# A transformer block on one core: 96 instead of 80 tokens on gathered expert rows, and routing in two groups of four heads

## Chip, cores and metric

The kernel runs on one core of a Trainium2 chip. The metric is the device time of one execution in microseconds (us), as the median of three runs.

## What is computed

One block: two attention branches merged into `x`, then a product-key expert layer over 256 tokens of width 1024. The change touches only the expert layer:

```python
def peer_ffn(h, w_q, sub_k1, sub_k2, expert_u, expert_v):
    q = (ht @ w_q).reshape(T, PEER_HEADS, PEER_QDIM)
    s1 = jnp.einsum('thd,nd->thn', q[..., :PEER_HALF], sub_k1)
    s2 = jnp.einsum('thd,nd->thn', q[..., PEER_HALF:], sub_k2)
    v1, i1 = lax.top_k(s1, PEER_TOPK)
    v2, i2 = lax.top_k(s2, PEER_TOPK)
    cand = v1[..., :, None] + v2[..., None, :]
    vals, pos = lax.top_k(cand, PEER_TOPK)
    experts = jnp.take_along_axis(cand_idx, pos, axis=-1)
    gates = jax.nn.softmax(vals, axis=-1)
...
        u = expert_u[ec]
        a = jnp.einsum('cd,chkd->chk', xc, u)
        w = jax.nn.gelu(a) * gc
        return jnp.einsum('chk,chkd->cd', w, expert_v[ec])
```

There are 8 heads, 128 keys a side, 16 experts per head and token, and 16,384 experts with a row of 1024 float32 in `expert_u` and one in `expert_v`.

## The kernel before

The tokens are handled in two ways. For the last ND = 176 tokens every expert is computed: 128 tiles of U (128 experts by 1024, 512 KB) give `ps_u` (`u_tile`, L581), ScalarE applies gelu into `ga`, the gates multiply `ga`, and 128 tiles of V accumulate into `acc` (L833). Each U or V tile costs eight matmuls with 176 columns. For the first NG = 80 tokens only the chosen rows are fetched: an indirect DMA (`fetch`, L601) brings one row of `expert_u` to each of 128 partitions, VectorE forms the dot products (L617), and later the same with rows of `expert_v`, which it accumulates in `accG` (L627). SETS = (64, 16) says how the 80 tokens are laid on partitions: 64 tokens with two partitions each, 16 with eight. So 80 fetches of U rows and 80 of V rows are needed, 512 KB each.

The order of the work, all in `block_kernel`:

- Query: 16 tiles of `wq` give `qT` (L649 to L652). VectorE splits each weight tile into a high and a low part (L102), two to three tiles ahead.
- Routing: the generator `retrieval(h)` (L658) handles one half of 128 tokens and all eight heads: scores on TensorE (L667), a copy on ScalarE (L669), then on VectorE two rounds of top-16 and the one-hot sums that turn positions into expert numbers (`tri`); a softmax with an Exp on ScalarE (L728); for h = 0 small DMAs on SP's queue that lay indices and gates out for the gathers (`gidx`, `gwt`, L742); last, three transposes on TensorE (L746) and four copies.
- U, tiles 0 to 53 (`TOPK_TILES`): after each tile the loop L761 takes `TOPK_PER_TILE` = 1.4 units from the generator, whose `yield`s are the units' costs, and, once `gidx` is under way, `STEPS_U` = 0.85 steps of the generator `gathers` (L598). One step consumes one gathered row. The scheduler keeps each engine's queue in order, so what stands ahead in a queue holds what stands behind it.
- U, tiles 54 to 127: the same with `gate_group` (L780) for four tokens at a time: one-hot tiles, eight matmuls into `ps_g` (L797), and the product with `ga`.
- V, tiles 0 to 127: eight matmuls each, then `mark` (L835), a VectorE read of one column of the tile that keeps the gather steps behind it in VectorE's queue, then `STEPS_V` = 0.65 steps.

```python
        raw = wp.tile([P, DM], F32, name="uvraw", tag=("wraw", "whi", "wlo")[i % 3])
...
            if n % 2 == 1:
                for m in (n + 3, n + 4):
                    if m < 2 * NG:
                        fetch(m)
```

The first line gives weight tiles nine buffers, so SP loads up to nine ahead; a buffer is free again when TensorE and `mark` have read it. The others keep four gathered rows in flight or waiting, and two new ones are fetched when a pair is used up. SP issues the weight loads, POOL the indirect ones; both use the same 16 DMA engines.

Of the kernel before, what the change touches and what calls it, by code (L numbers as in the profile page):

```python
# [8 lines left out]
F32 = mybir.dt.float32  # L9
# [20 lines left out]
PH = 8  # L30
TOPK = 16
# [14 lines left out]
TOPK_PER_TILE = 1.4  # L46
# [20 lines left out]
def block_kernel(ctx: ExitStack, tc, x, g2, consts, small, wqkv, wkv5, wmg, w1kv, wup, wout, wq, uT, u, v, folds, out):  # L67
# [30 lines left out]
    state = {"tokens": 0, "tiles": 0}  # L98
# [482 lines left out]
    def u_tile(i, raw):  # L581
        ps = bank("ps_u", "u", 3)[:, :ND]
        for c in range(NC):
            nc.tensor.matmul(ps, raw[:, c * P:(c + 1) * P], h2f[:, c, NG:], start=c == 0, stop=c == NC - 1)  # L584
# [13 lines left out]
    def gathers():  # L598
        slots = []

        def fetch(n):  # L601
            src = u if n < NG else vrows
            if n % 2 == 0:
                slots.append(hpool.tile([P, 2, DM], F32, name="grow", tag="h2lo" if n // 2 % 2 else "h2hi"))
            dst = slots[n // 2][:, n % 2]
            j = n % NG
            nc.gpsimd.indirect_dma_start(out=dst, out_offset=None, in_=src,  # L607
                                         in_offset=bass.IndirectOffsetOnAxis(ap=gidx[:, j:j + 1], axis=0))

        for n in range(4):  # L610
            fetch(n)
        for n in range(2 * NG):
            g = slots[n // 2][:, n % 2]
            j = n % NG
            k = sum(j >= sum(SETS[:m]) for m in range(1, len(SETS)))
            if n < NG:
                nc.vector.tensor_tensor_reduce(out=g, in0=g, in1=h2d[k], scale=1.0, scalar=0.0, op0=ALU.mult,  # L617
                                               op1=ALU.add, accum_out=gdot[:, j:j + 1])
                if j % GCH == GCH - 1:
                    r = slice(j + 1 - GCH, j + 1)  # L620
                    nc.scalar.activation(gdot[:, r], gdot[:, r], AF.Gelu_apprx_tanh)
# [10 lines left out]
            yield  # L632
# [4 lines left out]
    def gather_steps(rate):  # L637
        gdebt[0] += rate
        while gdebt[0] >= 1:
            gdebt[0] -= 1  # L640
            with tc.issue_after(state["dve"].ins):
                next(gather, None)

    with ExitStack() as ts:
# [4 lines left out]
        for i in range(16):  # L649
            ps = bank("ps_q", "u", 3)[:, :S]  # L650
            cols_proj(wq[i], ps, lambda c: (h2hi[:, c, :], h2lo[:, c, :]), lo_last=i == 0)
            nc.scalar.copy(qT[:, i, :], ps)  # L652

# [4 lines left out]
        def retrieval(h):  # L658
            sp = tk
            vals = sp.tile([P, 2, PH, TOPK], F32, name="tv")  # L660
            idx = sp.tile([P, 2, PH, TOPK], U32, name="ti")
            for w in range(2):
                sc = sp.tile([P, PH, P], F32, name="sc12")
                for q in range(2):
                    ps = pst.tile([P, 512], F32, name="ps_s12", tag="t", bufs=3).rearrange("p (h n) -> p h n", n=P)
                    for k in range(4):
                        nc.tensor.matmul(ps[:, k, :], qT[:, 2 * (4 * q + k) + w, h * P:(h + 1) * P],  # L667
                                         SM("k2T" if w else "k1T"), start=True, stop=True, skip_group_check=True)
                    nc.scalar.copy(sc[:, 4 * q:4 * q + 4], ps)  # L669
                yield 0.0  # L670
                for hh in range(PH):
                    state["dve"] = topk(nc, sp, vals[:, w, hh, :], idx[:, w, hh, :], sc[:, hh, :], P)
                    yield 1.0
            idf = sp.tile([P, 2, PH, TOPK], F32, name="idf")
            nc.vector.tensor_copy(idf, idx)
            cand = sp.tile([P, PH, NCAND], F32, name="cand")
            o = a = 0
            while a < TOPK:
# [15 lines left out]
            off = sp.tile([P, P], F32, name="off")
            inc = sp.tile([P, P], F32, name="inc")
# [7 lines left out]
            pb = sp.tile([P, P], F32, name="pb")  # L703
            nc.vector.tensor_sub(pb, pa, off)
            nc.vector.scalar_tensor_tensor(pb, pa, float(o + CAND_N[TOPK // 2 - 1]), pb, op0=ALU.is_lt, op1=ALU.mult)
            yield 2.6
            diff = sp.tile([P, PH, TOPK], F32, name="diff")
            nc.vector.tensor_copy(diff[:, :, 0:1], idf[:, 0, :, 0:1])
            nc.vector.tensor_sub(diff[:, :, 1:], idf[:, 0, :, 1:], idf[:, 0, :, :TOPK - 1])
            for w, (pos, op, table) in enumerate(((pa, ALU.is_ge, diff), (pb, ALU.is_equal, idf[:, 1]))):  # L710
                posb = sp.tile([P, PH, TOPK], BF16, name="posb")
                nc.vector.tensor_copy(posb.rearrange("p h j -> p (h j)"), pos)
                for q in range(2):
                    hs = slice(4 * q, 4 * q + 4)
                    oh = sp.tile([P, 4, TOPK, TOPK], BF16, name="oh", tag="oh")
                    nc.vector.tensor_tensor(oh, posb[:, hs].unsqueeze(2).to_broadcast([P, 4, TOPK, TOPK]),
                                            steps16[:, w].unsqueeze(1).to_broadcast([P, 4, TOPK, TOPK]), op=op)
                    nc.vector.tensor_mul(oh, oh, table[:, hs].unsqueeze(3).to_broadcast([P, 4, TOPK, TOPK]))
                    o2 = sp.tile([P, 4, TOPK // 2, TOPK], BF16, name="oh2", tag="oh2")
                    nc.vector.tensor_add(o2, oh[:, :, 0::2], oh[:, :, 1::2])  # L720
                    nc.vector.tensor_add(oh[:, :, 0:4], o2[:, :, 0::2], o2[:, :, 1::2])
                    nc.vector.tensor_add(o2[:, :, 0:2], oh[:, :, 0:4:2], oh[:, :, 1:4:2])
                    state["dve"] = nc.vector.tensor_add(tri[:, w, hs], o2[:, :, 0], o2[:, :, 1])
                    yield 2.6
            ex = sp.tile([P, PH, TOPK], F32, name="ex")
            nc.vector.tensor_sub(ex, tv, tv[:, :, 0:1].to_broadcast([P, PH, TOPK]))
            with tc.issue_after(state["act"].ins):
                nc.scalar.activation(ex, ex, AF.Exp)  # L728
            se = sp.tile([P, PH], F32, name="se")
            nc.vector.tensor_reduce(se, ex, axis=AX.X, op=ALU.add)  # L730
            nc.vector.reciprocal(se, se)
            nc.vector.scalar_tensor_tensor(tri[:, 2], ex, GSCALE, se.unsqueeze(2).to_broadcast([P, PH, TOPK]),
                                           op0=ALU.mult, op1=ALU.mult)
            if h == 0:
                tf = tri.rearrange("p i h j -> p i (h j)")
                ei = sp.tile([P, P], U32, name="ei")
                nc.vector.scalar_tensor_tensor(ei, tf[:, 0], float(NKEY), tf[:, 1], op0=ALU.mult, op1=ALU.add)
                for dst, src in ((gidx, ei), (gwt, tf[:, 2])):
                    for k, n in enumerate(SETS):
                        o = sum(SETS[:k])  # L740
                        for i in range(P // n):
                            nc.sync.dma_start(dst[i * n:(i + 1) * n, o:o + n], src[o:o + n, i * n:(i + 1) * n])  # L742
                state["rows"] = True
            pt = bank("ps_tri", "g")[:, :3 * P].rearrange("p (i t) -> p i t", t=P)
            for i in range(3):
                nc.tensor.transpose(pt[:, i, :], tri[:, i].rearrange("p h j -> p (h j)"), C("ident"))  # L746
# [221 lines left out]
```

## Time and profile before

| | us |
|---|---|
| median of 3 runs (lowest, highest) | 980.64 (980.05, 981.41) |
| profiled execution | 977.79 |
| its span, first to last instruction | 975.9 |
| TensorE busy in the span | 950.0 |
| VectorE busy | 577.1 |

The mean granted clock of TensorE is 0.993 of full speed. Over the span DMA moved 265 MB, 272 GB/s. Busy shares are means over stages that differ, so the stretches are read one by one. In the rows below PE is TensorE, PEld its weight loads, DVE VectorE, ACT ScalarE, POOL GpSimd, and SP the engine that issues the weight loads.

### The profile page before, as it was taken

The numbers are of one execution on the slowest core, as the hardware profiler recorded it, in microseconds if no ns is written. First come the engines' busy times: TensorE is split into PE (matmuls) and PEld (weight loads), VectorE is DVE, ScalarE is ACT, GpSimd is POOL, SyncE is SP. The second block draws the span as 40 slices with busy tenths as digits, with TensorE's granted clock in tenths as the row PEclk, the third lists the DMA queues.
The fourth block names the chain that finished last, engine by engine and source line by source line (L and its number), as shares of the span: only waits on it lengthen the run. The fifth ranks groups of instructions, "written<-read, shape, count | busy, mean of one in ns | idle before, by whom it ended". The sixth has DMA issues, their size and how long they took to land.

```text
span 975.9 us, 16945 instructions
## 1 busy us (share of the span) xinstructions
PE 950.0 (97%) x6465; PEld 903.5 (93%) x6465; DVE 577.1 (59%) x1575; ACT 313.6 (32%) x787; POOL 179.8 (18%) x185
## 2 busy tenths in 40 slices
PE   8999999999999999869999999999999999999998
PEld 6778758997999999869999999999999999999997
DVE  5887775586428849976777777764444344343201
ACT  6777776546431121025444544420000000000000
POOL 2000000002000023332232333224332323232000
PEclk9999999999999999989999999999999999999999
DMA  7665302567576589987999999999999999999751
GB/s 240 191 220 188 117 1 96 186 198 195 161 248 200 172 308 401 356 283 273 332 322 338 323 323 328 343 324 389 399 387 381 358 376 346 370 365 378 233 177 44
DMA packets 74448, 265.15 MB, mean 272 GB/s; under 512 B 9152, under 2 KB 9408, under 8 KB 74368
## 3 DMA queue, kind: packets, MB, share of 16 engines
q1 hardware_dynamic: 50512, 177.61, 51.4%
q0 software_dynamic: 23856, 86.47, 25.1%
q8 instruction: 51, 0.84, 0.3%
q14 instruction: 29, 0.24, 0.1%
HBM read 261.86 MB, written 1.05 MB: 269 GB/s over the span
## 4 chain that ended last, share of the span: by engine, by line
PE 86%; DVE 5%; DMA 5%; ACT 2%; issue 1%; POOL 0%; SPq 0%; ACTq 0%
PE acc L833 31%; PE ps_u L584 26%; PE ps_g L797 4%; DMA grow<-in_u_dram,gidx 2%; PE ps_q L117 2%; PE ps_mg L120 2%; PE ps_mg L117 2%; PE ps_q L118 2%; PE ps_mg L118 2%; PE ps_s L406 2%; PE ps_q L120 1%; DMA wraw<-in_wqkv_dram 1%; DVE grow L617 1%; PE ps_proj L167 1%; PE ps_pt L423 1%; PE ps_proj L165 1%
## 5 line engine op out<-in xcount | busy, mean ns | idle before, releaser
L584 PE MATMUL ps_u<-h2f,uvraw 128*128 128x176 f32 x2048 | 319.4, 316 | 2.6 <-ACT ga L588 2.6
L584 PEld LDWEIGHTS ps_u<-h2f,uvraw 128*128 128x128 f32 x2048 | 311.1, 193 | 2.9 <-ACT ga L588 2.8
L833 PE MATMUL acc<-ga,uvraw 128*128 128x176 f32 x2048 | 305.7, 313 | 0.0
L833 PEld LDWEIGHTS acc<-ga,uvraw 128*128 128x128 f32 x2048 | 305.5, 190 | 0.0
L607 POOL DMA_INDIRECT grow<-in_u_dram,gidx x80 | 85.8, 1073 | 296.8 <-DVE gdot L617 150.9
L102 DVE TENSOR_TENSOR wlo<-wraw,whi 128x1024 fp32r<-128x1024 f32 (+1 forms) x80 | 95.6, 1197 | 42.5 <-ACT whi L101 42.1
L627 DVE SCALAR_TENSOR_TENSOR accG<-grow,gwt,accG 128x1024 f32<-128x1024 f32 x78 | 99.9, 1281 | 35.0 <-DMA grow<-in_v_dram,gidx 34.6
L607 POOL DMA_INDIRECT grow<-in_v_dram,gidx x80 | 81.9, 1024 | 188.9 <-DVE accG L627 113.6
L835 DVE COPY mark<-uvraw 128x1 f32<-128x1 f32 x128 | 19.5, 152 | 150.2 <-DMA uvraw<-in_v_dram 147.2
L617 DVE CUSTOM_DVE_ANT_0 grow<-grow,h2d 128x1024 f32<-128x1024 f32 x80 | 97.4, 1218 | 12.5 <-DMA grow<-in_u_dram,gidx 12.2
L101 ACT CAST whi<-wraw 128x1024 fp32r<-128x1024 f32 (+1 forms) x80 | 82.0, 1029 | 67.8 <-PE ps_q L118 18.4
L846 ACT COPY accT<-acc 128x352 f32<-128x352 f32 x2 | 0.9, 452 | 304.7 <-PE acc L833 304.7
L588 ACT ACTIVATE ga<-ps_u 128x176 f32<-128x176 f32 (+35 forms) x124 | 33.9, 275 | 181.9 <-PE ps_u L584 170.2
L792 ACT ACTIVATE og<-o,gT 128x128 f16<-128x128 f16 x176 | 67.3, 566 | 17.4 <-PE ps_g L797 14.2
L797 PE MATMUL ps_g<-og,o 128*128 128x128 f16 x352 | 48.5, 295 | 0.0
L592 DVE TENSOR_TENSOR ga<-ga,au 128x176 f32<-128x176 f32 (+35 forms) x74 | 18.8, 255 | 41.2 <-ACT au L591 36.4
L797 PEld LDWEIGHTS <-o 128*128 128x128 f16 x352 | 40.0, 116 | 2.0
L164 PE MATMUL ps_proj<-whi,hhi 128*128 128x512 f32 (+1 forms) x96 | 36.4, 382 | 2.3 <-ACT whi L101 1.5
L165 PE MATMUL ps_proj<-whi,hlo 128*128 128x512 f32 (+1 forms) x96 | 35.7, 377 | 0.0
L117 PE MATMUL ps_mg<-hhi,whi 128*128 128x256 f32 x128 | 32.3, 288 | 0.0
L117 PE MATMUL ps_q<-h2hi,whi 128*128 128x256 f32 x128 | 31.6, 284 | 0.7 <-ACT qTp L652 0.5
L118 PE MATMUL ps_mg<-hlo,whi 128*128 128x256 f32 x128 | 31.9, 285 | 0.0
(256 smaller groups left out, 1103.6 us busy)
## 6 DMA issues: line engine op xcount, KB each, us to landing
uvraw<-in_uT_dram SPq DMA_DIRECT2D x128, 512.0 KB
uvraw<-in_v_dram SPq DMA_DIRECT2D x128, 512.0 KB
wraw<-in_wqkv_dram SPq DMA_DIRECT2D x20, 512.0 KB
wraw<-in_wmg_dram SPq DMA_DIRECT2D x16, 512.0 KB
wraw<-in_wq_dram SPq DMA_DIRECT2D x16, 512.0 KB
wraw<-in_w1kv_dram SPq DMA_DIRECT2D x8, 512.0 KB
wraw<-in_wup_dram SPq DMA_DIRECT2D x8, 512.0 KB
wraw<-in_wout_dram SPq DMA_DIRECT2D x8, 512.0 KB
```

The source lines that it names most:

```text
L101: nc.scalar.copy(hi, src)
L102: state["dve"] = nc.vector.tensor_sub(lo, src, hi)
L117: nc.tensor.matmul(ps, lh, rh, start=i == 0, stop=False)
L118: nc.tensor.matmul(ps, ll if lo_last else lh, rh if lo_last else rl, start=False, stop=False)
L165: nc.tensor.matmul(ps(h), ll, hi[:, r], start=False, stop=False)
L584: nc.tensor.matmul(ps, raw[:, c * P:(c + 1) * P], h2f[:, c, NG:], start=c == 0, stop=c == NC - 1)
L607: nc.gpsimd.indirect_dma_start(out=dst, out_offset=None, in_=src, in_offset=bass.IndirectOffsetOnAxis(ap=gidx[:, j:j + 1], axis=0))
L617: nc.vector.tensor_tensor_reduce(out=g, in0=g, in1=h2d[k], scale=1.0, scalar=0.0, op0=ALU.mult, op1=ALU.add, accum_out=gdot[:, j:j + 1])
L627: nc.vector.scalar_tensor_tensor(accG[:, k], g, gwt[:, j:j + 1], accG[:, k], op0=ALU.mult, op1=ALU.add)
L792: nc.scalar.activation(og[0][:, :, k], o1[:, :, k], AF.Copy, scale=gT[:, t0 + k:t0 + k + 1])
L797: nc.tensor.matmul(ps[:, k, :], o2[:, :, k], og[i][:, :, k], start=i == 0, stop=i == 1, skip_group_check=True)
L833: nc.tensor.matmul(acc[c // 2][:, c % 2, 0:ND], raw[:, c * P:(c + 1) * P], ga_at(i), start=i == 0 and c % 2 == 0, stop=i == NKEY - 1, skip ...
```

## The change

- NG becomes 96 (SETS = (64, 32)), so ND becomes 160 and each fetch count 96. Matmuls on `u` and `acc` have 160 columns, there are 40 gate groups instead of 44.
- `retrieval(h, hg, tri)` handles four heads (QH = 4) and runs four times. The first two groups belong to h = 0, and each lays out its own half of `gidx` and `gwt`; `state["rows"]` says how many fetches are covered, and `gather_steps` stays six behind it until all are.
- The generator starts beside query tile 8 (`TOPK_PER_Q` = 1.0 a tile), then takes 1.1 units per U tile, over 60 tiles instead of 54. Gather steps: 0.55 a tile in these, 0.8 in the other U tiles, 0.9 in V.
- The transposes and copies become `route(h, tri)`. That of h = 0 is emitted after the third group, that of h = 1 two units after the fourth, each behind the latest U matmul.

```diff
-TOPK_TILES = 54
-SETS = (64, 16)
+TOPK_TILES = 60
+SETS = (64, 32)
...
-STEPS_U = 0.85
-STEPS_V = 0.65
+STEPS_R = 0.55
+STEPS_U = 0.8
+STEPS_V = 0.9
...
-TOPK_PER_TILE = 1.4
+TOPK_PER_TILE = 1.1
+TOPK_PER_Q = 1.0
...
     def gather_steps(rate):
-        gdebt[0] += rate
-        while gdebt[0] >= 1:
+        gdebt[0] += rate if "rows" in state else 0.0
+        while gdebt[0] >= 1 and (state["rows"] == NG or state["steps"] + 6 <= state["rows"]):
             gdebt[0] -= 1
+            state["steps"] += 1
...
+        def route(h, tri):
+            with tc.issue_after(state["pe"].ins):
+                pt = bank("ps_tri", "g")[:, :3 * P].rearrange("p (i t) -> p i t", t=P)
+                for i in range(3):
+                    nc.tensor.transpose(pt[:, i, :], tri[:, i].rearrange("p h j -> p (h j)"), C("ident"))
...
         def both():
+            tris = [tk.tile([P, 3, PH, TOPK], F32, name="tri") for _ in range(NH)]
             for h in range(NH):
-                yield from retrieval(h)
+                for hg in range(HG):
+                    yield from retrieval(h, hg, tris[h])
+                    if h == 1 and hg == 0:
+                        route(0, tris[0])
+                        yield 0.8
+            yield 2.0
+            route(1, tris[1])
+            yield 0.8
...
+        for i in range(16):
+            ps = bank("ps_q", "u", 3)[:, :S]
+            cols_proj(wq[i], ps, lambda c: (h2hi[:, c, :], h2lo[:, c, :]), lo_last=i == 0)
+            state["act"] = nc.scalar.copy(qT[:, i, :], ps)
+            if i >= PH:
+                topk_steps(TOPK_PER_Q)
...
             u_tile(i, ahead.pop(0))
-            debt -= TOPK_PER_TILE
...
-            if "rows" in state:
-                gather_steps(STEPS_U)
+            topk_steps(TOPK_PER_TILE)
+            gather_steps(STEPS_R)
```

TensorE's queue at the end of the routing, before. `ps_s` are scores, `ps_u` U tiles (eight rows each), `ps_tri` the transposes, `o_...` the first weights of a gate group:

```order
L667 MATMUL ps_s_4043<-sml,qTp 128x128 x4
L667 MATMUL ps_s_4049<-sml,qTp 128x128 x4
L584 MATMUL ps_u<-h2f,uvraw 128x176 x152
L746 MATMUL ps_tri<-cst,tri 128x128 x2
L584 MATMUL ps_u<-h2f,uvraw 128x176 x12
L746 MATMUL ps_tri<-cst,tri 128x128
L584 MATMUL ps_u<-h2f,uvraw 128x176 x12
L797 LDWEIGHTS o_4562
```

And with the change:

```order
L588 MATMUL ps_u<-h2f,uvraw 128x160 x96
L751 MATMUL ps_tri<-cst,tri 128x128 x3
L588 MATMUL ps_u<-h2f,uvraw 128x160 x8
L668 MATMUL ps_s_4341<-sml,qTp 128x128 x4
L588 MATMUL ps_u<-h2f,uvraw 128x160 x24
L668 MATMUL ps_s_4409<-sml,qTp 128x128 x4
L588 MATMUL ps_u<-h2f,uvraw 128x160 x112
L751 MATMUL ps_tri<-cst,tri 128x128 x3
L588 MATMUL ps_u<-h2f,uvraw 128x160 x8
L819 LDWEIGHTS o_4745
```

The transposes of h = 0 now stand far behind their group's scores, with the third group's U tiles between; those of h = 1 stand together, one U tile ahead of the first gate group.

SP's queue from the first U loads to the first V load, before (`gidx` and `gwt` are the small transfers that lay indices and gates out):

```order
L578 DMA uvraw<-in_uT_dram 128x1024 x26
L742 DMA gidx<-ei 64x64 x2
L742 DMA gidx<-ei 16x16 x8
L578 DMA uvraw<-in_uT_dram 128x1024 x9
L742 DMA gwt<-tri 64x64 x2
L742 DMA gwt<-tri 16x16 x8
L578 DMA uvraw<-in_uT_dram 128x1024 x93
```

And with the change:

```order
L582 DMA uvraw<-in_uT_dram 128x1024 x12
L743 DMA gidx<-ei 64x32 x2
L743 DMA gidx<-ei 32x16 x4
L582 DMA uvraw<-in_uT_dram 128x1024 x6
L743 DMA gwt<-tri 64x32 x2
L743 DMA gwt<-tri 32x16 x4
L582 DMA uvraw<-in_uT_dram 128x1024 x14
...
L582 DMA uvraw<-in_uT_dram 128x1024 x2
...
L582 DMA uvraw<-in_uT_dram 128x1024 x94
```

The first `gidx` stands behind 12 loads instead of 26, and a second set of small transfers (left out) follows behind 32 and 34 loads.

## Rows read from the trace of the kernel before

**Rows 1.** The page: busy time per engine (share) xinstructions; the chain's shares by line.

```profile
PE 950.0 (97%) x6465; PEld 903.5 (93%) x6465; DVE 577.1 (59%) x1575; ACT 313.6 (32%) x787; POOL 179.8 (18%) x185
...
PE acc L833 31%; PE ps_u L584 26%; PE ps_g L797 4%; DMA grow<-in_u_dram,gidx 2%; PE ps_q L117 2%; PE ps_mg L120 2%; PE ps_mg L117 2%; PE ps_q L118 2%; PE ps_mg L118 2%; PE ps_s L406 2%; PE ps_q L120 1%; DMA wraw<-in_wqkv_dram 1%; DVE grow L617 1%; PE ps_proj L167 1%; PE ps_pt L423 1%; PE ps_proj L165 1%
```

**Rows 2.** Windows: stretch, length, busy time per engine (instructions), clock, DMA share, GB/s.

```profile
370.00:395.00 25.00, 25.00 (x173) 25.00 (x173) 23.56 (x130) 4.34 (x12) 6.70 (x7) 1.00 1.02 400
657.00:697.00 40.00, 40.00 (x270) 40.00 (x270) 19.66 (x30) 0.63 (x2) 16.43 (x16) 1.00 1.01 387
700.00:740.00 40.00, 40.00 (x270) 40.00 (x269) 17.64 (x32) 0.00 (x0) 12.95 (x12) 1.00 1.01 390
...
288.06:435.00 146.94, 135.60 (x910) 134.59 (x910) 112.36 (x551) 28.25 (x69) 30.84 (x27) 0.97 0.82 293
...
659.50:965.00 305.50, 305.50 (x2050) 305.50 (x2049) 107.47 (x198) 0.77 (x2) 72.65 (x72) 1.00 0.89 331
```

**Rows 3.** TensorE's groups and the waits at the end of the routing.

```profile
L746 PE MATMUL ps_tri<-cst,tri 128*128 128x128 f32 x6 | 1.8, 325 | 8.8 <-DVE tri L732 7.5 <-DVE tri L723 1.2
...
PE ps_u L584 <- ACT ga L588: 2.6, 1, 2.6
```

**Rows 4.** The chain in order of time (start, us, what) at 424 us.

```profile
424.68 8.36 DMA grow<-in_u_dram,gidx
...
434.44 0.30 DVE tri L732
...
434.79 0.47 PE ps_tri L746
```

**Rows 5.** Waits from 659.5 to 965 us (total, times, longest).

```profile
DVE mark L835 <- DMA uvraw<-in_v_dram: 143.8, 84, 4.6
...
DVE accG L627 <- DMA grow<-in_v_dram,gidx: 34.6, 22, 4.9
```

**Rows 6.** VectorE's timeline: the first mark of V.

```profile
645.76 0.15 DVE L835 COPY mark<-uvraw 128x1 f32<-128x1 f32 x1 [2.50 <-DMA uvraw<-in_v_dram]
```

**Rows 7.** The chain in order of time: query, U, scores, gates, V, the end.

```profile
287.10 0.96 PE ps_q L120 x8
288.06 2.39 PE ps_u L584 x16
290.45 1.78 PE ps_s L667 x16
...
444.78 0.94 PE ps_g L797 x8
...
659.52 305.49 PE acc L833 x2048
965.01 3.43 PE fin L843 x8
968.44 3.59 PE fin L850 x32
```

**Rows 8.** VectorE's windows beside the query tiles and in L617 alone; two of its groups.

```profile
260.00:288.06 28.06, 9.21 (x8) 1.00 0.63 202
...
357.80:435.00 77.20, 29.63 (x49) 0.95 0.91 339
...
L702 DVE TENSOR_TENSOR off<-off,inc 128x128 f32<-128x128 f32 x12 | 3.4, 284 | 0.0
...
L723 DVE TENSOR_TENSOR tri<-oh 128x64 f32<-128x64 bf16 x8 | 1.7, 218 | 0.0
```

**Rows 9.** The DMA view from 700 to 860 us.

```profile
DMA packets 16184, 59.06 MB, mean 369 GB/s; under 512 B 1795, under 2 KB 1795, under 8 KB 16172
```

**Rows 10.** Windows of 1 us, TensorE alone: around two waits; busy time, clock, DMA share, GB/s.

```profile
238.00:239.00 1.00, 0.00 (x0) 1.00 0.92 206
...
240.00:241.00 1.00, 0.76 (x8) 1.00 0.98 127
...
408.00:409.00 1.00, 1.00 (x5) 0.50 1.00 397
```

More of the change, by code (lines that the diff above doesn't have):

```diff
@@ L30 @@
 PH = 8
+HG = 2
+QH = PH // HG
 TOPK = 16
@@ L96, in block_kernel @@
     x1 = hpool.tile([P, NH, DM], F32, name="x1")
-    state = {"tokens": 0, "tiles": 0}
+    state = {"tokens": 0, "tiles": 0, "steps": 0}
     def split(hi, lo, src):
@@ L583, in u_tile @@
         for c in range(NC):
-            nc.tensor.matmul(ps, raw[:, c * P:(c + 1) * P], h2f[:, c, NG:], start=c == 0, stop=c == NC - 1)
+            state["pe"] = nc.tensor.matmul(ps, raw[:, c * P:(c + 1) * P], h2f[:, c, NG:], start=c == 0, stop=c == NC - 1)
         dst = ga_at(i)
@@ L614, in gathers @@
             j = n % NG
-            k = sum(j >= sum(SETS[:m]) for m in range(1, len(SETS)))
+            k = sum(j % (NG // HG) >= sum(SETS[:m]) // HG for m in range(1, len(SETS)))
             if n < NG:
@@ L623, in gathers @@
                                                    op0=ALU.mult, op1=ALU.mult)
-            elif j == sum(SETS[:k]):
+            elif k not in begun:
+                begun.add(k)
                 nc.vector.tensor_scalar(accG[:, k], g, gwt[:, j:j + 1], None, op0=ALU.mult)
@@ L648, in block_kernel @@
         qT = tk.tile([P, 16, S], F32, name="qTp", bufs=1)
[L649 to L652, printed above, removed]
         steps16 = tk.tile([P, 2, TOPK, TOPK], BF16, name="steps16", bufs=1)
@@ L709, in retrieval @@
             nc.vector.tensor_sub(diff[:, :, 1:], idf[:, 0, :, 1:], idf[:, 0, :, :TOPK - 1])
+            hs = slice(QH * hg, QH * hg + QH)
             for w, (pos, op, table) in enumerate(((pa, ALU.is_ge, diff), (pb, ALU.is_equal, idf[:, 1]))):
-                posb = sp.tile([P, PH, TOPK], BF16, name="posb")
+                posb = sp.tile([P, QH, TOPK], BF16, name="posb")
                 nc.vector.tensor_copy(posb.rearrange("p h j -> p (h j)"), pos)
[L713 to L724, printed above, removed]
@@ new lines, in retrieval @@
+                o2 = sp.tile([P, QH, TOPK // 2, TOPK], BF16, name="oh2", tag="oh2")
+                nc.vector.tensor_add(o2, oh[:, :, 0::2], oh[:, :, 1::2])
+                nc.vector.tensor_add(oh[:, :, 0:4], o2[:, :, 0::2], o2[:, :, 1::2])
+                nc.vector.tensor_add(o2[:, :, 0:2], oh[:, :, 0:4:2], oh[:, :, 1:4:2])
+                state["dve"] = nc.vector.tensor_add(tri[:, w, hs], o2[:, :, 0], o2[:, :, 1])
+                yield 2.2
+            ex = sp.tile([P, QH, TOPK], F32, name="ex")
@@ L733, in retrieval @@
                                            op0=ALU.mult, op1=ALU.mult)
             if h == 0:
[L735 to L738, printed above, removed]
+                ei = sp.tile([P, QH, TOPK], U32, name="ei")
+                state["dve"] = nc.vector.scalar_tensor_tensor(ei, tri[:, 0, hs], float(NKEY), tri[:, 1, hs],
+                                                              op0=ALU.mult, op1=ALU.add)
@@ L739, in retrieval @@
+                for dst, src in ((gidx, ei), (gwt, tri[:, 2, hs])):
+                    src = src.rearrange("p h j -> p (h j)")
                     for k, n in enumerate(SETS):
-                        o = sum(SETS[:k])
+                        o, m = sum(SETS[:k]), n // HG
+                        c = hg * (NG // HG) + o // HG
                         for i in range(P // n):
-                            nc.sync.dma_start(dst[i * n:(i + 1) * n, o:o + n], src[o:o + n, i * n:(i + 1) * n])
-                state["rows"] = True
@@ L744, in retrieval @@
-            pt = bank("ps_tri", "g")[:, :3 * P].rearrange("p (i t) -> p i t", t=P)
-            for i in range(3):
-                nc.tensor.transpose(pt[:, i, :], tri[:, i].rearrange("p h j -> p (h j)"), C("ident"))
+                            nc.sync.dma_start(dst[i * n:(i + 1) * n, c:c + m], src[o:o + n, i * m:(i + 1) * m])
+                state["rows"] = (hg + 1) * NG // HG
+            yield 0.4
+        def route(h, tri):
[3 more added lines that the diff above has]
+                    nc.tensor.transpose(pt[:, i, :], tri[:, i].rearrange("p h j -> p (h j)"), C("ident"))
```

77 lines of the change are left out of this document (40 added, 37 removed).

## The prediction

> **What bounds the kernel now.** I read the page first, then the windows by stage, then the chain, then the waits and the DMA views.
>
> TensorE is busy for 97% of the span, and two lines carry over half of the chain that ended last [rows 1]: `acc` L833 with 31% and `ps_u` L584 with 26%. The reader is to see there that only shorter TensorE work, or fewer stalls of it, can shorten this kernel. Both multiply weight tiles by 176 columns of tokens. The trace has 2,048 passes for a stage of 128 tiles [rows 7], sixteen a tile, so one matmul of the code is two passes.
>
> The windows by stage [rows 2] show two kinds of stretch. From 659.5 to 965.0 us (the V stage: `acc`) TensorE is never idle. In the stretch that holds the routing, from 288.06 to 435 us, it is busy for 135.6 of 146.9 us, and its mean clock is 0.97. What ended those idle times is in the waits [rows 3]: the routing transposes L746 waited 7.5 and 1.2 us for VectorE's `tri`, and `ps_u` waited 2.6 us for ScalarE, in whose queue a step waits for VectorE's dot products. The chain at 424 us [rows 4] says why VectorE was late: it waited 8.4 us for a gathered row that stands in its queue ahead of the last softmax step. So the first U tiles are bound by VectorE and its gathers, the rest by TensorE's columns.
>
> What nearly binds as well is DMA. In V it moves 331 GB/s over the whole stage, and in its filled stretches 387 and 390 GB/s at a share of 1.01 [rows 2]. VectorE's waits in V are for transfers [rows 5]: `mark` waits 143.8 us for weight tiles, which is harmless because they land ahead of their use. The first mark stands at 645.76 us [rows 6], V's first matmul at 659.52 [rows 7]: 13.8 us, some six tiles ahead.
>
> **The change, part by part.**
>
> *Columns.* ND falls from 176 to 160. A pass takes 305.49 us / 2048 = 149.2 ns at 176 columns; the same float32 passes take 3.43 / 8 = 429 ns at 512 columns and 3.59 / 32 = 112 ns at 128 [rows 7]. On the line from 176 to 512 sixteen columns are worth 13.3 ns, on the line from 128 to 176 12.3. I take the first, since it is nearer to what a clean stream pays: 135.9 ns, a tile of 2.174 us where it was 2.387. That is 27.3 us less in U (25.2 by the other line) and, if TensorE stays the bound, 27.3 us less in V.
>
> *Gate groups.* 40 groups of four tokens instead of 44, at 0.94 us of TensorE each [rows 7]: 3.8 us less. Scores and transposes keep their number.
>
> *The routing stall.* U runs from 288.06 to 659.52 us [rows 7], 371.5 us. In it lie 2048 x 149.2 ns = 305.5, 44 x 0.94 = 41.4, 64 score passes at 1.78 / 16 = 7.1, and six transposes at 0.3 = 1.8 [rows 3, 7]. What is left, 16 us, is stalls and the slow clock behind them. The change starts VectorE's routing beside the query tiles, where VectorE is now busy for 9.2 of 28.1 us [rows 8], and queues each half's transposes later. VectorE's work before the last transposes: 112.4 us busy in that stretch less 29.6 us of gathers [rows 2, 8] = 83 us of routing, plus some 4 us (an estimate: 33 small steps a group, issued four times rather than twice, at about 60 ns of fixed cost, from 284 ns at 128 elements and 218 at 64 [rows 8]), plus 28 gathers at 1.2 us and eight splits at 1.2 us [rows 8]: 130 us. The time for it, from query tile 8 to the transposes behind U tile 58, is 8 x 2.88 us (24 passes at 0.96 / 8 [rows 7]) + 59 x 2.174 + 8 for scores = 159 us. So it fits, with less room near the end, where five reductions stand ahead of the last softmax step, each behind a gather. I leave 5 us of the 16; bounds 0 and 16. Saved: 11 us. The cover here is that room; if gathers take it, the last transposes are late again.
>
> *Queues.* SP now issues the first index transfers after 12 U loads and not 26, and sits behind `ei` with the 13th load. `ei` of the first group is due near U tile 5 and tile 12 is used 26 us after U's start, so I cost it at nothing. POOL meets `accT`'s memset after 86 gathers rather than 90; the 87th row is wanted at the tenth mark of V, so this waits for nothing new. Four Exp table changes instead of two are ScalarE's, busy for 28 of 147 us there [rows 2].
>
> *More gathers.* Each of 192 rows (before 160) is 0.524 MB like a weight tile. By the rates in the code 28 are used in the first 60 U tiles and 55 in the other 68, so 83 by the end of U (before 88 of 160), and 109 are left for V at 0.9 a tile, the last at V tile 121. In U this needs at most 1.55 x 0.524 MB / 2.174 us = 374 GB/s: it just fits. In V it needs 1.9 x 0.524 / 2.174 = 458 GB/s, and that does not fit: the highest rate that these stretches hold is 400, for 25 us [rows 2]. So V, today bound by TensorE, becomes bound by DMA.
>
> Its length: at V's start some six tiles have landed and 87 rows are fetched. To V tile 121 that leaves 116 tiles and 105 rows, 221 x 0.5243 = 115.9 MB. At 393 GB/s, between the filled 40 us stretches (387, 390) and the 25 us one (400), it is 295 us; then come the landing and six to seven tiles at 2.174, 15 us: 310 us. Bounds: 305 at 400 GB/s, 314.5 at 387. Against 305.5 now, V gets 4.5 us *longer* though its matmuls are 27.3 us shorter. VectorE, busy for 107 of 305.5 us there now [rows 2], has room for half as many steps again.
>
> Here a rule speaks against the change. The Trainium skill (DMA: Bandwidth & Descriptors, Specifications) gives about 358 GB/s as one core's share of HBM; by that the 115.9 MB take 324 us, V 339 and the run 972 us. The trace differs from it, with 387 to 400 GB/s held, so it has no part in my sum.
>
> *Sum.* 975.9 (span) - 27.3 - 3.8 - 11 + 4.5 = 938.3 us of span. The profiled execution took 977.8 us, 1.9 more than its span, so 940.2; the median of the runs shown, 980.64, is 2.85 above it, so **943 us** in the runs.
>
> **Rivals.**
>
> *TensorE stays the bound in V.* V takes 128 x 2.174 = 278 us, 32 less: 911 us. For it: weights are now ready six tiles ahead. Against: it needs 458 GB/s for 265 us, and no stretch holds that.
>
> *DMA in V holds only its mean.* From 700 to 860 us it moved 369 GB/s at shares near full [rows 9]. At that 115.9 MB take 314 us, V 329: 962 us. For it: random rows and weight tiles mix as they do there. Against: there the gathers were paced by VectorE's marks, so the engines were not always asked.
>
> *Routing late again.* The last transposes wait as now, for gathers ahead of the softmax step: 16 us of stall instead of 5, 954 us. For it: the 8.4 us gather of [rows 4], in a stage that will ask for 374 GB/s. Against: the room of 29 us worked out above.
>
> *Slower: the clock falls in V.* TensorE will wait for weights in V for the first time. After its wait of 2.6 us near 404 us [rows 3] the granted clock was 0.50 (1.2 GHz) in the window at 408 us [rows 10]. At 1.2 GHz a tile takes 4.35 us, longer than the 2.5 us between transfers, so TensorE would bind and lose time. With V at 349 us the gain is used up: that is when 26% of its tiles run at the low level; at 35%, V takes 376 us and the run 1009. Against: the waits come to 32 us over 128 tiles, mostly 0.4 us a tile, and after a wait of about 2 us near 238.5 us the clock stayed at 1.00 [rows 10]. The Trainium skill (TensorE: Matmul & The Clock Gate, HAM oscillation) describes this failure for loops that wait on DMA at every step; the two rows show one wait with it and one without.
>
> **Chances.** My forecast, V bound by DMA near 393 GB/s and a small stall: 0.62 (933 to 959 us by its bounds). TensorE-bound V 0.08; DMA at its mean 0.12; late routing 0.14; clock 0.04. The range reaches from 920 to 962: it holds the forecast, late routing and most of the case at 369 GB/s, and leaves out TensorE-bound V and the clock. A measurement of this kernel can tell about 0.2% from no change, 2 us. Faster by more than that are all cases but the last: 0.94; a mild form of the clock case lands within 0.2%: 0.02; slower 0.04.
>
> **What would show it.** In the changed profile: about 136 ns per pass where nothing waits; V between 305 and 315 us, with TensorE idle in it by some 30 us put down to `uvraw` from the V table; DMA near 390 GB/s from V's start to its last gather, and VectorE's `mark` waiting far less than 143.8 us, its accumulations far more than 34.6 [rows 5]. U should be near 329 us, and the transposes should wait for `tri` by under 5 us. I am wrong about DMA if V takes 280 us or 330, about the clock if the granted clock in V is below 0.95, and about routing if the transposes wait over 10 us.

## The result, and the profile after

| | before | after |
|---|---|---|
| median of the runs made side by side (lowest, highest) | 980.35 (978.66, 981.41) | 941.18 (938.46, 945.49) |
| profiled execution | 977.79 | 938.46 |
| its span | 975.9 | 936.7 |

The ratio is 0.9606, with a 95% interval of 0.9567 to 0.9645. The forecast was 943 us with a range of 920 to 962. Where the time went is a sum of four stretches, each from the first matmul of one stage to that of the next. After the change they are read here, in the view of single lines (durations min/median/max in ns, first and last start in us):

```profile
L588 PE MATMUL ps_u<-h2f,uvraw x2048: 297/299/317, 289.2 to 611.1; 128*128 128x160 f32 x187
...
L855 PE MATMUL acc<-ga,uvraw x2048: 299/299/403, 611.2 to 925.2; 128*128 128x160 f32 x187
```

| stretch | before [rows 7] | after | difference |
|---|---|---|---|
| up to U | 288.06 | 289.2 | +1.1 |
| U | 371.5 | 322.0 | -49.5 |
| V | 305.5 | 314.2 | +8.7 |
| end of V to end of span | 10.9 | 11.3 | +0.4 |

So U gave 49 us, V gave 9 us back. The page of the changed kernel (busy time per engine, then the chain that ended last, by engine and by line) answers to [rows 1]:

```profile
PE 900.6 (96%) x6433; PEld 842.9 (90%) x6433; DVE 614.3 (66%) x1663; ACT 309.6 (33%) x768; POOL 218.4 (23%) x213
...
PE 56%; DMA 28%; issue 7%; POOL 3%; DVE 3%; ACT 2%; DVEq 0%; POOLq 0%; ACTq 0%; SPq 0%
PE ps_u L588 28%; DMA grow<-in_v_dram,gidx 21%; PE ps_g L819 4%; POOL grow L611 3%; DMA grow<-in_u_dram,gidx 3%; PE ps_q L121 2%; PE ps_mg L124 2%; PE ps_mg L121 2%; PE ps_q L124 2%; PE ps_q L122 2%; PE ps_mg L122 2%; PE ps_s L410 2%; PE ps_proj L171 1%; PE ps_pt L427 1%; DVE wlo L106 1%
```

Before, `acc` alone carried 31% of the chain. Now the chain of V runs over DMA: `grow` from the V table carries 21% of the span, and `acc` is no longer among the leading lines. The groups (busy us, mean ns of one, idle time before them and its releaser) say the same from TensorE's side:

```profile
L855 PE MATMUL acc<-ga,uvraw 128*128 128x160 f32 x2048 | 292.9, 302 | 21.3 <-DMA uvraw<-in_v_dram 19.5
L855 PEld LDWEIGHTS acc<-ga,uvraw 128*128 128x128 f32 x2048 | 279.9, 190 | 34.2 <-DMA uvraw<-in_v_dram 32.3
L588 PE MATMUL ps_u<-h2f,uvraw 128*128 128x160 f32 x2048 | 287.3, 299 | 0.0
...
L751 PE MATMUL ps_tri<-cst,tri 128*128 128x128 f32 x6 | 1.0, 273 | 0.0
```

The last two rows have no idle time at all: the transposes, which waited 8.8 us [rows 3], wait for nothing, and neither does `ps_u`. By stage (length, busy time per engine, clock, DMA share, GB/s), beside [rows 2]:

```profile
289.00:430.00 141.00, 141.00 (x1051) 140.68 (x1050) 118.55 (x546) 39.02 (x97) 34.33 (x32) 1.00 0.92 349
430.00:611.00 181.00, 181.00 (x1376) 179.72 (x1375) 137.38 (x370) 89.33 (x321) 54.67 (x52) 1.00 0.95 345
...
660.00:700.00 40.00, 37.15 (x262) 35.46 (x261) 19.12 (x29) 0.00 (x0) 15.55 (x14) 1.00 0.95 362
700.00:900.00 200.00, 183.82 (x1271) 173.61 (x1269) 96.48 (x151) 0.00 (x0) 80.14 (x72) 1.00 1.01 394
...
611.00:926.00 315.00, 293.67 (x2053) 280.45 (x2052) 151.63 (x254) 1.37 (x4) 119.80 (x109) 1.00 0.99 385
```

TensorE is never idle in U, and the clock is 1.00 in all these stretches, V's idle times included. Over 200 us of V, DMA moves 394 GB/s, over all of V 385. The waits (total, times, longest):

```profile
DVE accG L633 <- DMA grow<-in_v_dram,gidx: 136.9, 93, 3.7
...
PEld acc L855 <- DMA uvraw<-in_v_dram: 32.3, 51, 2.2
```

VectorE's accumulations wait 136.9 us where they waited 34.6, and `mark`, which waited 143.8 [rows 5], no longer stands among the long waits (3.4 us in all). What paces V now is in the chain in order of time, from 718 to 740 us:

```profile
717.99 8.72 DMA grow<-in_v_dram,gidx
...
726.81 0.06 DVE accG L633
726.87 1.14 issue
728.01 0.16 DVE mark L857
...
728.36 0.94 POOL grow L611
729.30 0.30 issue
729.60 7.41 DMA grow<-in_v_dram,gidx
...
739.90 7.44 DMA grow<-in_v_dram,gidx
```

This is a closed loop: rows land, VectorE adds them, POOL fetches the next pair into the buffers, they land. One turn takes 11.6 and 10.3 us. Two pairs turn at once, so four rows per turn, 2.6 to 2.9 us a row. The rows by VectorE's lines (first and last start at the end; L631 takes the first row of each of the two sets):

```profile
L633 DVE SCALAR_TENSOR_TENSOR accG<-grow,gwt,accG x94: 1283/1285/1346, 657.7 to 922.6; 128x1024 f32<-128x1024 f32 x94
L631 DVE TENSOR_SCALAR accG<-grow,gwt x2: 752/752/753, 655.7 to 745.3; 128x1024 f32<-128x1024 f32 x2
```

One of the two rows of L631 lies between the first and the last of L633, so 264.9 us hold 94 rows: 2.82 us a row. It is counted so in every run below.

### The profile page after: what moved, and what is told of

The parts are those of the page before. It is cut to its first block, busy times and chain, and to the rows that moved or that the text cites. A ratio compares the mean times of both kernels' runs of the same rounds, so it can differ in the third digit from the quotient of the medians.

```text
span 936.7 us, 17034 instructions
## 1 busy us (share of the span) xinstructions
PE 900.6 (96%) x6433; PEld 842.9 (90%) x6433; DVE 614.3 (66%) x1663; ACT 309.6 (33%) x768; POOL 218.4 (23%) x213
## 4 chain that ended last, share of the span: by engine, by line
PE 56%; DMA 28%; issue 7%; POOL 3%; DVE 3%; ACT 2%; DVEq 0%; POOLq 0%; ACTq 0%; SPq 0%
PE ps_u L588 28%; DMA grow<-in_v_dram,gidx 21%; PE ps_g L819 4%; POOL grow L611 3%; DMA grow<-in_u_dram,gidx 3%; PE ps_q L121 2%; PE ps_mg L124 2%; PE ps_mg L121 2%; PE ps_q L124 2%; PE ps_q L122 2%; PE ps_mg L122 2%; PE ps_s L410 2%; PE ps_proj L171 1%; PE ps_pt L427 1%; DVE wlo L106 1%
## 5 line engine op out<-in xcount | busy, mean ns | idle before, releaser
L855 PE MATMUL acc<-ga,uvraw 128*128 128x160 f32 x2048 | 292.9, 302 | 21.3 <-DMA uvraw<-in_v_dram 19.5
L855 PEld LDWEIGHTS acc<-ga,uvraw 128*128 128x128 f32 x2048 | 279.9, 190 | 34.2 <-DMA uvraw<-in_v_dram 32.3
L588 PE MATMUL ps_u<-h2f,uvraw 128*128 128x160 f32 x2048 | 287.3, 299 | 0.0
L588 PEld LDWEIGHTS ps_u<-h2f,uvraw 128*128 128x128 f32 x2048 | 280.7, 190 | 0.1
L633 DVE SCALAR_TENSOR_TENSOR accG<-grow,gwt,accG 128x1024 f32<-128x1024 f32 x94 | 120.8, 1285 | 137.0 <-DMA grow<-in_v_dram,gidx 136.9
L611 POOL DMA_INDIRECT grow<-in_u_dram,gidx x96 | 102.1, 1063 | 302.2 <-DVE gdot L622 149.1
L611 POOL DMA_INDIRECT grow<-in_v_dram,gidx x96 | 106.0, 1104 | 166.0 <-DVE mark L857 150.0
L622 DVE CUSTOM_DVE_ANT_0 grow<-grow,h2d 128x1024 f32<-128x1024 f32 x96 | 116.7, 1218 | 34.6 <-DMA grow<-in_u_dram,gidx 34.5
L592 ACT ACTIVATE ga<-ps_u 128x160 f32<-128x160 f32 (+32 forms) x124 | 33.5, 271 | 143.7 <-PE ps_u L588 143.4
L596 DVE TENSOR_TENSOR ga<-ga,au 128x160 f32<-128x160 f32 (+32 forms) x68 | 16.8, 247 | 23.4 <-ACT au L595 22.9
```

The costliest lines, as they stand in the source:

```text
L588: state["pe"] = nc.tensor.matmul(ps, raw[:, c * P:(c + 1) * P], h2f[:, c, NG:], start=c == 0, stop=c == NC - 1)
L855: nc.tensor.matmul(acc[c // 2][:, c % 2, 0:ND], raw[:, c * P:(c + 1) * P], ga_at(i), start=i == 0 and c % 2 == 0, stop=i == NKEY - 1, skip ...
```

## The experiments

**The two parts alone.** First the columns, with the routing as before (e1_cols, an edit of the kernel before):

```diff
-SETS = (64, 16)
+SETS = (64, 32)
-STEPS_V = 0.65
+STEPS_V = 0.9
```

> The kernel before with 96 tokens on gathered rows and 0.9 gather steps per V tile; routing, transposes and the other rates stay as they were. Theory A (VectorE sets the pace of the routing tiles): the 54 routing tiles get 11.5 us shorter on TensorE but VectorE's work there stays, so the stall grows from 16 to about 27 us, U takes 352 us; V is bound by DMA, about 307 us; 962 us in the runs. Rival (the stall is a fixed 16 us): U 340 us, 950 us in the runs.

Measured: 961.72 us, ratio 0.9836 [0.9784, 0.9887]. The time is A's, but not by A's sum: U takes 344.8 us (288.4 to 633.2) and not 352, V 312 and not 307. The contents of U, as summed in the prediction, are 278.3 + 37.6 + 7.1 + 1.8 = 324.8, so the stall is 20 us, neither the 16 of the rival nor the 27 of A. The waits of TensorE in U (total, times, longest) are for ScalarE's `ga` and VectorE's `tri`, as before, and for a gate group's `og`:

```profile
PE ps_u L584 <- ACT ga L588: 7.7, 1, 7.7
PE ps_g L797 <- DVE og L793: 4.7, 1, 4.7
PE ps_tri L746 <- DVE tri L723: 2.2, 1, 2.2
```

Then the routing, with 176 columns (e2_routing, an edit of the changed kernel):

```diff
-SETS = (64, 32)
+SETS = (64, 16)
-STEPS_V = 0.9
+STEPS_V = 0.65
```

> The changed kernel with 80 tokens (64 and 16) and 0.65 steps per V tile as before: the new routing without the new columns. Theory A: the 16 us of stall in U go, V stays bound by TensorE at 305.5 us: 964 us in the runs. Rival (four groups cost VectorE and the queues what the early start gives): 975 to 980 us, with TensorE idle in the routing tiles as before.

Measured: 965.23 us, ratio 0.9848 [0.9828, 0.9868]. U takes 353.1 us, and TensorE waits nowhere in it. V is bound by TensorE as before:

```profile
L855 PE MATMUL acc<-ga,uvraw 128*128 128x176 f32 x2048 | 305.7, 313 | 0.0
```

The parts give 18.6 and 15.1 us, both together 39.2. The intervals of the runs leave the 5.5 us between open, but in U the traces show 4.4 of them: 26.7 us and 18.4 us alone, 49.5 together. Shorter tiles alone come with a stall that is 4 us longer; with the new routing that is gone too.

**What in the routing does it.** Without the early start (e7_late):

```diff
-TOPK_PER_TILE = 1.1
+TOPK_PER_TILE = 1.25
...
-            if i >= PH:
-                topk_steps(TOPK_PER_Q)
```

> The changed kernel with the routing begun at U's first tile instead of query tile 8, at 1.25 instead of 1.1 units a tile; two groups and late transposes stay. Theory A (the early start gives VectorE its room): TensorE waits again near the last transposes and for ScalarE, 5 to 12 us, 946 to 953 us. Rival (the late queueing of the transposes alone removes the stall): U stays at 322 to 324 us, 941 us.

Measured: 951.56 us, 0.9707 [0.9676, 0.9737]. The time is in A's range, the waits are not: U takes 328.1 us, 6 more, and 1.8 of these are score passes that now stand in U. TensorE waits only once there:

```profile
PE ps_tri L751 <- DVE tri L731: 2.9, 1, 2.9
```

In the profiled execution, 12.9 us longer, V takes 1 us more and what follows it 5.5. With the transposes queued at once (e11_now):

```diff
-            with tc.issue_after(state["pe"].ins):
+            if True:
...
-                    if h == 1 and hg == 0:
-                        route(0, tris[0])
-                        yield 0.8
-            yield 2.0
-            route(1, tris[1])
-            yield 0.8
+                route(h, tris[h])
+                yield 0.8
```

> The changed kernel with each half's transposes queued as soon as its second group is emitted, not behind a later U matmul; the early start and the two groups stay. Theory A (VectorE's room took the stall away, not the later place of the transposes): U grows by at most 3 us, 940 to 945 us in the runs. Rival (the later place does it): the transposes wait for tri by 8 us or more, 949 us or more.

Measured: 943.07 us, 0.9629 [0.9594, 0.9664], which can't be told from the change itself. U takes 323.5 us, 1.5 more, with one short wait for `tri`:

```profile
PE ps_tri L751 <- DVE tri L731: 1.1, 1, 1.1
```

So the early start is worth 6 us of U, and the place of the transposes 1.5. Neither carries most of the gain: with the same columns and the old routing (e1_cols) U takes 344.8 us, 22.8 more than in the change, and of these 16.7 are saved without the early start and 21.3 without the late queueing. What both runs keep is the two groups of four heads, 60 routing tiles instead of 54, and 0.55 gather steps a tile beside them instead of 0.85. Which of the three it is, or whether the early start and the late queueing can stand in for each other, was not run. The traces point to the tiles: the last `tri` starts at 425.1 us in e1_cols, 422.4 in the change and 427.8 in e7_late, so VectorE is hardly done sooner, while TensorE has six tiles more ahead of the last transposes. That is argued, not shown.

**Half the bytes of one stream.** If V lasts as long as its bytes take (theory A, the prediction's), halving either stream must free TensorE. In e3_half_weights 64 of V's tiles are loaded and each is used twice:

```diff
-            ahead.append(load_raw(v, i + len(ahead)))
+            m = i + len(ahead)
+            if m % 2 == 0:
+                vtile = load_raw(v, m // 2)
+            ahead.append(vtile)
```

> The changed kernel with only 64 tiles of V loaded, each used for two neighbouring steps of the accumulation; the output leaves out the other 64. All gathered rows are still fetched. Theory A (V is bound by bytes of DMA): 33.6 MB fewer, so V falls to TensorE's own 278 to 283 us, 908 us in all. Rival (V is bound by the round trip of gathered rows through their four buffers and VectorE's order): V stays above 300 us, 930 us or more.

Measured: 922.17 us, 0.9403 [0.9344, 0.9462], between A's 908 and the rival's 930. TensorE's part comes out as A says: 278.4 us without a wait. The run does not. The rows end after TensorE does, with DMA far from its 394 GB/s, as a window of V shows:

```profile
640.00:880.00 240.00, 240.00 (x1769) 240.00 (x1768) 122.65 (x189) 0.22 (x1) 102.36 (x92) 1.00 0.87 307
```

The wait of the last stage for those rows:

```profile
PE fin L868 <- DVE mark L860: 10.2, 1, 10.2
```

And VectorE's rows, by their line (first and last start at the end):

```profile
L633 DVE SCALAR_TENSOR_TENSOR accG<-grow,gwt,accG x94: 1274/1285/1287, 659.7 to 901.3; 128x1024 f32<-128x1024 f32 x94
```

241.6 / 94 = 2.57 us a row at 307 GB/s, against 2.82 at 394. Half the weights gave the rows a tenth only: the loop of the chain, not the bytes, is what is left. Behind its wait of 10.2 us the last stage also runs at a lower granted clock (0.73 over the 20 us below). It takes 24.1 us where it takes 11.3 in the change, 2.6 more than the wait:

```profile
900.00:920.00 20.00, 8.78 (x38) 5.73 (x38) 6.35 (x16) 0.00 (x0) 0.00 (x0) 0.73 0.16 59
```

In e4_half_rows only the first V row of each pair is fetched and used twice:

```diff
+            if n >= NG and n % 2:
+                return
...
-            g = slots[n // 2][:, n % 2]
+            g = slots[n // 2][:, n % 2 if n < NG else 0]
```

> The changed kernel with only the first V row of each pair fetched and used twice; the output leaves out half of the V rows, VectorE's steps stay. Theory B (bytes): about 50 rows, 26 MB, fewer in V; V falls to TensorE's 278 to 282 us with nearly no wait for weights, 903 to 909 us. Rival (V is held by VectorE's in-order steps and marks): V stays above 300 us.

Measured: 921.32 us, 0.9392 [0.9346, 0.9438]. A, which its expectation calls theory B, fails here: V takes 299.0 us though half its rows' bytes are gone, just under the rival's bound of 300, and DMA is not full in its window:

```profile
640.00:900.00 260.00, 247.81 (x1767) 243.65 (x1767) 130.65 (x210) 0.21 (x1) 52.63 (x50) 0.99 0.89 318
```

VectorE waits for rows all the same:

```profile
DVE accG L635 <- DMA grow<-in_v_dram,gidx: 118.1, 40, 7.9
```

Its 94 steps between 657.8 and 908.7 us take 2.67 us each, and two steps use one row. With one row of a pair in flight instead of two, the loop is hardly shorter.

**The rates.** More gathers in U, so fewer are left for V (e5_u10):

```diff
-STEPS_U = 0.8
+STEPS_U = 1.0
```

> The changed kernel with 1.0 instead of 0.8 gather steps per tile in the U tiles that carry gates: 13 to 14 rows move from V into U. Theory A (bytes bound V, U has room: 2.0 x 0.524 MB / 2.74 us = 383 GB/s): V loses 6.8 MB, 17 us, U stays at 322 us; 924 us in the runs. Rival (U is short of DMA as well): U grows by what V loses, 941 us.

Measured: 947.69 us, 0.9662 [0.9646, 0.9679], slower than the change, not faster, and slower than the rival's 941. U takes 5 us more (327.2). V takes 316.9, though it has 13 rows less. The last V row starts at 899.2 us, and behind it TensorE has tiles left while DMA has nothing to do:

```profile
920.00:940.00 20.00, 20.00 (x135) 18.09 (x134) 1.81 (x4) 0.85 (x2) 0.00 (x0) 1.00 0.00 1
```

From this came theory B: `mark` ties the streams together. A mark stands in VectorE's queue behind its rows and holds a weight buffer, so while rows last a tile takes the step rate times a row's time; only what remains after the last row goes at TensorE's 2.17 us. A row's time B still takes from bytes at 393 GB/s, (1 + rate) x 0.5243 MB a tile. By B a lower rate in V, with a few more rows in U, must help (e8_u09_v08):

```diff
-STEPS_U = 0.8
-STEPS_V = 0.9
+STEPS_U = 0.9
+STEPS_V = 0.8
```

> The changed kernel with 0.9 instead of 0.8 steps per gate tile of U and 0.8 instead of 0.9 per tile of V, so that the last row falls on the last V tiles. Theory B (a V tile with rows beside it takes (1 + rate) x 0.5243 MB / 393 GB/s, one without rows 2.17 us, and DMA that is idle after the last row is lost): 1.8 x 0.5243 / 0.393 = 2.40 us a tile, V 296 to 302 us, U 323 to 325 us, 926 to 932 us in the runs. Rival (V is held by the round trip of the rows in their four buffers): rows come no faster than 2.6 to 2.8 us each, 103 rows, V 285 us or less, but a late row still holds the marks, so V 305 to 314 us and 935 to 941 us.

Measured: 935.03 us (931.60 to 936.33), 0.9529 [0.9511, 0.9546]. This is the fastest kernel here that does the whole work, and its interval lies below that of the change. U costs no more (322 us). V's tiles take 295.5 us, as B has it, but then the last stage waits 8 us for the last rows, and runs 3 us longer behind that wait, so the run lies 3 us above B's range, at the edge of the rival's. The time alone doesn't decide between them. A window of V shows the tiles' share of TensorE:

```profile
700.00:900.00 200.00, 195.52 (x1379) 188.12 (x1378) 93.99 (x154) 0.00 (x0) 75.26 (x70) 1.00 1.03 407
```

The waits of TensorE in V and behind it:

```profile
PE fin L865 <- DVE mark L857: 8.0, 1, 8.0
...
PE acc L855 <- DMA uvraw<-in_v_dram: 5.2, 11, 1.3
```

A rate between the two (e12_u09_v085):

```diff
-STEPS_U = 0.8
-STEPS_V = 0.9
+STEPS_U = 0.9
+STEPS_V = 0.85
```

> 0.9 steps per gate tile of U as in the run with 0.9 and 0.8, but 0.85 per V tile, so that the last row falls on V tile 121. Theory B (the same bytes, DMA full to nearly the end): the 8 us wait of the last matmuls for rows goes, TensorE's waits in V grow by as much: 932 to 937 us, no different from 0.8. Rival (the rows' pace is what binds, so asking earlier for them ends them earlier): 927 us or less.

Measured: 944.55 us over six runs (939.57 to 950.18), 0.9638 [0.9602, 0.9673]. B's range is missed by 8 us, the rival's by 18: V takes 315.6 us, and a row 275.7 / 94 = 2.93 us. Why 0.85 makes rows slower than 0.8 is open.

A rate far higher (e10_v12):

```diff
-STEPS_V = 0.9
+STEPS_V = 1.2
```

> The changed kernel with 1.2 instead of 0.9 steps per V tile: the same bytes, earlier. Theory B (pace by rate): rows end at tile 91, 85 tiles at 2.93 us, 37 at 2.17 us: V 335 to 345 us, 962 to 972 us. Rival (only the sum of bytes counts): V 310 to 316 us, 941 us.

Measured: 1009.04 us, 1.0282 [1.0255, 1.0308]. B has the direction; its size was some 40 us short. The rows of V's line give its length, 383 us:

```profile
L855 PE MATMUL acc<-ga,uvraw x2048: 299/299/637, 612.3 to 995.3; 128*128 128x160 f32 x187
```

VectorE's rows, by their line:

```profile
L633 DVE SCALAR_TENSOR_TENSOR accG<-grow,gwt,accG x94: 1274/1285/1286, 658.6 to 928.3; 128x1024 f32<-128x1024 f32 x94
```

A third more rows a tile did not bring the rows faster: 2.87 us each, with the last 6 us *later* than in the change. B had put a row at 2.93 / 1.2 = 2.44 us, and that is the term that failed: with 2.87 a tile with its rows takes 3.44 us. So the tiles fell back, and 67 us of them stand behind the last row. DMA moves less, and the clock falls as well, in the two windows:

```profile
660.00:920.00 260.00, 192.57 (x1187) 179.90 (x1186) 120.84 (x163) 0.00 (x0) 108.13 (x92) 0.92 0.92 329
880.00:900.00 20.00, 15.02 (x74) 14.38 (x75) 9.20 (x13) 0.00 (x0) 10.18 (x8) 0.73 0.94 320
```

Still more tokens on rows, 112 (e6_112):

```diff
-SETS = (64, 32)
+SETS = (64, 32, 16)
-STEPS_U = 0.8
-STEPS_V = 0.9
+STEPS_U = 0.9
+STEPS_V = 1.0
```

> The changed kernel with 112 tokens on gathered rows (64, 32 and 16), 0.9 steps per gate tile of U and 1.0 per V tile. Theory B (bytes bind): 32 more rows are 16.8 MB, 42 us at 400 GB/s, against 27 us fewer on TensorE in each stage; U 296 to 305 us, V 335 to 350 us, 945 to 965 us. Rival (fewer columns still shorten it as from 80 to 96): 920 us or less.

Measured: 1038.19 us, 1.0583 [1.0542, 1.0624], slower than the kernel before. B had 945 to 965 us, so its direction from the change is right and its size is far off. U takes 319.6 us, where 296 to 305 were expected, and waits there for weights too. V's tiles take 379 us, and DMA moves 335 GB/s. Then the last stage still waits for rows, which take 331.5 / 110 = 3.01 us each. The waits of TensorE:

```profile
PE acc L855 <- DMA uvraw<-in_v_dram: 93.9, 78, 3.4
PE ps_u L588 <- DMA uvraw<-in_uT_dram: 16.3, 2, 10.8
PE fin L865 <- DVE accG L633: 15.3, 1, 15.3
PE fin L865 <- DVE mark L857: 11.9, 1, 11.9
```

**The hold of late marks.** ScalarE copies the column as soon as the tile has landed, and `mark` reads the copy, so a late mark no longer holds a weight buffer (e9_actmark):

```diff
-        state["dve"] = nc.vector.tensor_copy(mark, raw[:, 0:1])
+        seen = dp.tile([P, 1], F32, name="seen", bufs=12)
+        nc.scalar.copy(seen, raw[:, 0:1])
+        state["dve"] = nc.vector.tensor_copy(mark, seen)
```

> The changed kernel, where ScalarE reads the column of each V tile and VectorE's mark reads ScalarE's copy: the pacing stays, but a late VectorE no longer holds a weight buffer. Theory B (bytes): nothing changes, V 314 us, 941 us. Rival (late marks hold the nine weight buffers and so delay loads, seen from 660 to 700 us where DMA's share was 0.95): V 300 to 308 us, 928 to 935 us.

Measured: 945.01 us, 0.9641 [0.9608, 0.9673], no gain on the change. But the wait has moved. TensorE's V takes 290.5 us instead of 314.2, and then waits for the rows:

```profile
PE fin L867 <- DVE mark L859: 20.5, 1, 20.5
```

290.5 + 20.5 = 311, and a row takes 2.81 us, as in the change. The hold on the buffers is real, and it is not what sets the end: the rows are.

The time of a V row, from the first and last start of `accG`'s accumulations, beside DMA's rate in a long window of V:

| kernel | rows a tile | us a row | GB/s (window) |
|---|---|---|---|
| after | 0.9 | 2.82 | 394 (700-900) |
| e8_u09_v08 | 0.8 | 2.86 | 407 (700-900) |
| e9_actmark | 0.9 | 2.81 | 402 (700-900) |
| e5_u10 | 0.9 | 2.86 | 389 (700-900) |
| e12_u09_v085 | 0.85 | 2.93 | 390 (700-900) |
| e10_v12 | 1.2 | 2.87 | 329 (660-920) |
| e6_112 | 1.0 | 3.01 | 335 (660-940) |
| e3_half_weights | 0.9 | 2.57 | 307 (640-880) |
| e4_half_rows | 0.9 | 2.67 a step | 318 (640-900) |

A step on a row costs 2.6 to 3.0 us whatever the rate and whatever DMA moves.

## Why the prediction was right, point by point

- **Columns.** 135.9 ns a pass was forecast; sixteen passes that wait for nothing take 2.18 us in the changed kernel's chain, 136 ns. The price read off the line between 176 and 512 columns held, and so did the 3.8 us of the gate groups: e1_cols contains both, and its U is 26.7 us shorter in spite of a longer stall.
- **The routing stall.** Mis-sized: 11 of 16 us were to go, all went. The 5 us kept back for "the room near the end" were not needed. 141 of 141 us are busy in the stretch where 135.6 of 146.9 were [rows 2]. The prediction's reason, VectorE's room from the early start, is shown for the smaller part only: without it U is 6 us longer (e7_late), against 22.8 with the old routing. The room was also worked out too large. The two rows behind the 60 ns, 284 ns at 128 elements and 218 at 64 [rows 8], give a fixed cost of 152 ns as they stand, so the small steps add 10 us rather than 4 and the room is 23 us rather than 29. And the 8.4 us of [rows 4] are one gather's time from issue to landing, not VectorE's wait for it: from 415 to 436 us VectorE waited 5.9 us in four waits, none over 1.9. A quarter of the score passes, 1.8 us, now stand ahead of U as well; the stretch up to U is 1.1 us longer.
- **V becomes longer though its matmuls are shorter.** 4.5 us longer was forecast, 8.7 was measured: 314.2 us against 310, inside the bounds of 305 and 314.5. That it came so near is in part luck. The rows' part was put at 295 us, 115.9 MB at 393 GB/s; the last row starts 311.4 us after V's first matmul, and over V some 121 MB moved at 385. The 15 us behind it were 3. One error is 16 us up, the other 12 down. The forecast named where it shows: 393 GB/s (394 over 200 us), TensorE idle by some 30 us (314.2 less the 278.4 of an undisturbed V in e3_half_weights is 35.8), and `accG` waiting far longer than `mark`. The traces keep speaking against a sum by about 358 GB/s (the Trainium skill, DMA: Bandwidth & Descriptors, Specifications): 394 over 200 us in the changed kernel, 407 in e8_u09_v08. Another page of the Trainium skill, HBM Reference (Specifications (TRN2)), takes that figure for a core's share and says that a core that streams alone goes well above it, and there the traces agree.
- **The reason, "V becomes bound by DMA", is the step that holds only in part.** A sum of bytes over a rate has one bound, and the runs show a second close behind it, the loop of the four row buffers, which the prediction does not price. With half of either stream's bytes gone, A has V bound by TensorE at 278 us, 36 less; V with its last rows took 288.6 (e3_half_weights, 278.4 + 10.2) and 299.0 us (e4_half_rows). A row's loop, 2.57 us even on engines at 307 GB/s, and the bytes, 2.81 us at 394 (0.9 rows and one tile of 0.5243 MB each, 1.107 MB a row), lie 9% apart. The changed kernel's 2.82 us a row agree with the bytes, but e10_v12 took 2.87 with DMA at 329, so its trace can't tell the two apart. The sum by bytes took the longer of two near equals, and so its number held while its use for the next step (e5_u10, e6_112) did not.
- **"Then come six to seven tiles at 2.174"** also failed: 3 us stand behind the last row, not 15. The marks fall behind TensorE and hold buffers, so the tiles drift back to the rows in the whole of V: when the last row starts, 122 marks are done, as the rate has it, but TensorE has begun 127 of 128 tiles.
- **The rivals.** TensorE-bound V did not come about, with 21.3 us of idle time at `acc`. DMA at 369 GB/s did not: 362 stands in 40 us alone (660 to 700), 385 over V. Late routing did not. The clock did not fall in the change (1.00, waits up to 2.2 us); it did in e10_v12, where waits reached 3.7 us and the mean of 260 us is 0.92. That rival's mechanism exists, at a rate of 1.2 rows a tile. (Its gain is used up with V at 310 + 37.6 = 347.6 us; the 349 is some 1 us high.)
- **The sum.** Span 938.3 forecast, 936.7 measured: U 7.4 us shorter than forecast (322.0 against 329.4), V 4.2 longer, the rest 1.5 longer. The errors partly cancel.

Open: which part of the new routing takes most of the stall away; how a turn of the row loop divides into issue, waiting in queues and transfer; why rows slow to 2.93 and 3.01 us at 0.85 and 1.0 rows a tile; and how much of the 40 us by which B missed e10_v12 is the clock. More row buffers, which would test the loop directly, were not tried.

## What to carry to other kernels

When work is moved from TensorE to gathered rows, price the rows twice: by their bytes at the rate that a filled stretch holds, and by their loop (land, use, refill) over the number of buffers. Halving a stream shows the second bound. Here it lay 9% behind the first, so that half the rows' bytes freed 15 us of the 36 that the bytes alone had promised. Where an in-order engine interleaves two streams by a fixed rate, a rate above what the gathers can deliver brings no row sooner; it only holds the other stream back and leaves it standing behind the last row. Of the steps that hide long vector work, an earlier start on a free engine was worth 6 us here and a later place for the result in the queue 1.5; taking one part away at a time did not find the part that carries most.

## What had not been expected

- Rates of 0.9 and 1.2 rows a tile end the V rows within 6 us of each other (922.6 and 928.3 us), and the runs differ by 68 us.
- DMA's share is a rough measure of what it moves: it stands at 0.92 with 329 GB/s in e10_v12, and at 1.03 with 407 in e8_u09_v08.
- Marks that no longer hold weight buffers freed TensorE by 24 us and the run by nothing.
